# TensorE's order in an expert stage written into the source: whole rounds, additions at two points, alternating accumulator banks, and the group of four experts last

## The chip, the cores and the metric

One core of a Trainium2 chip runs the whole kernel in one launch. The metric is the device time of that core in microseconds (us). Engines are named as the profile names them: PE is TensorE (PEld its weight loads), DVE is VectorE, ACT is ScalarE, POOL is GpSimd, SP is SyncE, which here only issues transfers.

## The reference

One layer of a diffusion backbone works on 256 latent tokens of width 1024: modulation, a combined input projection, a convolution branch, a recurrent branch, a merge, and then a mixture of experts. The change touches the last part alone. A router picks one of four groups for each token and two of the four experts in it, and each of 16 experts is a SwiGLU block (1024 to 512 and back to 1024):

```python
for g in range(N_GROUPS):
    sl = slice(g * EXPERTS_PER_GROUP, (g + 1) * EXPERTS_PER_GROUP)
    hg = jnp.einsum("nd,edf->nef", h, w_gate[sl])
    hu = jnp.einsum("nd,edf->nef", h, w_up[sl])
    act = jax.nn.silu(hg) * hu * combine[:, sl, None]
    out = out + jnp.einsum("nef,efd->nd", act, w_down[sl])
```

`combine` is zero but for a token's two experts. The result is added to the stream, and a final RMSNorm gives the output. Everything is in float32.

## The kernel before

The first 376 us do all that comes ahead of the experts. The expert stage then brings the weights of all 16 experts from HBM once, 16 times 6 MB, and computes with gathered tokens only.

**Groups and parts.** Experts are ranked by their number of tokens, except for experts 8 to 11, which are fixed in the source (`STATIC`) and come first. A group is a set of experts that share one pass: `groups` is the fixed group of four and then what `RANKS` lists by the rank of its first expert. Rank 8 means a group of four experts with 32 token slots each; the others are groups of two. Ranks 0 and 1, the fullest, get 128 slots each and the rest of the pairs 64, so a *part*, one pass over 128 slots, holds 4 x 32 or 2 x 64 slots. The group of ranks 0 and 1 has two parts, which read the same weights; all other groups have one. The order before is: fixed, 0, 8, 6, 2, 4.

**A part.** `up` (line L1228) computes the gate product and then the up product: for each of eight rounds k, the two (four) experts of the group each multiply their 64 (32) slots with a slice of their own weights, side by side in 64 (32) columns of the PE. A *round* is those two or four matmuls; in the trace each is two passes, so a group's gate product is 32 (64) passes. `swiglu` (L1182 to L1184) makes the activation on ACT and DVE, `turned` (L1250) transposes it in four matmuls, ACT copies it to `at` (L1275), and `down` (L1241) multiplies it with the down weights into two banks, one for each half c of the 1024 columns. `to_slots` (L1177) transposes the slot matrix `sg`, and `slot_weights` (L1260) fetches the routing weights. `scatter` makes `yv` (DVE, L1194), `yh` (ACT, L1197) and `yl` (DVE, L1198) for each half, and `add` (L1211, L1212) multiplies them back to the token rows, four matmuls for a half, and adds these to `xt`. The last part has no `yh` and `yl`; its additions are followed by squares for the final norm.

**Gathers.** `slots_of` (DVE, L999) builds the slot matrix, and `gather` fills `hg`, the tokens' columns: two matmuls for the row factors (L1011), 32 for the columns (L1025) through four `misc` banks of which two exist, a multiplication for each bank on DVE (L1029) and two bias additions for each on ACT (L1031). One gather serves ranks 0 and 1, one ranks 2 to 5, one ranks 6 to 11, and one the fixed group.

**Weights.** Each of the 96 halves of an expert matrix is a transfer of 1 MB, here a *chunk*, and goes to one of 18 buffers. The order of the chunks is the order of the groups, within a group gate, up, down, and of each the lower half before the upper. Chunk n waits for the release of the buffer that chunk n - 18 held. `load` is called where the program is done with earlier chunks; SP issues the 24 chunks of the fixed group (L596), POOL the other 72 as indirect transfers (L597), each queue in its order. A chunk of the group with two parts is free only when its second part has read it.

**What sets the order.** The framework's scheduler places the instructions of the expert stage by its own model of time; within an engine the program keeps that place. Only what is passed to `pin` (`tc.keep_in_program_order`) stands in the order of the source, and before this is the router and the fixed group's gather alone. So the scheduler decides where additions of one part fall among the rounds of the next, and where a gather is broken up. Banks: `up` uses `accum(0)` = `acca`, for the second part also `accb`, and `down` always `accb`, two banks each.

The loop at the end of the stage, before:

```python
for p in range(len(groups)):
    if p == 0:
        slots_for(p + 1)
    then = group(p, parts)
    if 0 < p < len(groups) - 1:
        slots_for(p + 1)
    if p + 1 == len(groups):
        gains()
        then()
    else:
        parts = parts_of(p + 1)
        then()
```

`group` runs `up` and `swiglu`, `parts_of` gathers, `then` is the rest of the group (`turned` to `add`); `gains` (L1335) spreads the final norm's factors.

Of the kernel before, what the change touches and what calls it, by code (L numbers as in the profile page):

```python
# [22 lines left out]
CAP = 64  # L23
# [16 lines left out]
RANKS = (0, 8, 6, 2, 4)  # L40
# [5 lines left out]
def hybrid_block(ctx: ExitStack, tc: tile.TileContext, a, out):  # L46
# [959 lines left out]

    def gather(dst, sg, ns, kb, first=False):

        pr = side_bank((128, ns))
        for b in range(2):  # L1010
            ins = T.matmul(pr, r2s[b].to_broadcast([128, 128]), sg[:, b].bitcast(F32), start=(b == 0), stop=(b == 1))  # L1011
            if first:
                pin(ins)
# [6 lines left out]
        for k0 in range(0, 8, kb):  # L1020
            pt = bank("accb", 2, (128, kb, ns)) if first and k0 // kb % 2 else misc((128, kb, ns))
            ks = range(k0, k0 + kb)
            for i, k in [(i, k) for i in range(4) for k in ks] if first else [(i, k) for k in ks for i in range(4)]:
                src, b = terms[i]
                ins = T.matmul(pt[:, k - k0], src[:, b, k, :], sg[:, b], start=(i == 0 and not (first and k > k0)),  # L1025
                               stop=(i == 3 and not (first and k < ks[-1])))
                if first:
                    pin(ins)
# [50 lines left out]
    V.scalar_tensor_tensor(pos, pc[:, 0:2], 1.0, mk16, op0=ALU.add, op1=ALU.mult)  # L1079
    sg0 = slots_of((pos[:, :, STATIC[0]:STATIC[0] + 4], CAP // 2), first=True)  # L1080
# [92 lines left out]
    def to_slots(st, sg):  # L1173

        pst = misc((128, 2, 128))
        for b in range(2):
            T.transpose(pst[:, b, :], sg[:, b].bitcast(F32), ident)  # L1177
# [9 lines left out]
    def scatter(od, st, ws, sums):  # L1187

        yvs = [tmp([128, 512], name="yv") for _ in range(2)] if sums else [None, None]
        for c in range(2):  # L1190
            if not sums:
                yvs[c] = tmp([128, 512], name="yv")
            yv = yvs[c]
            V.scalar_tensor_tensor(yv, od[c], ws, gt2[:, 512 * c:512 * c + 512], op0=ALU.mult, op1=ALU.mult)  # L1194
            if not sums:
# [3 lines left out]
                add(c, [(st, yh), (st, yl)])  # L1199
        if sums:  # L1200
            for c in range(2):
                add(c, [(st.bitcast(F32), yvs[c])])
                for b in range(2):
                    square(b, c)

    def add(c, ops):
        cs = slice(512 * c, 512 * c + 512)
        for b in range(2):
            po = side_bank()
            for i, (s_, y) in enumerate(ops):  # L1210
                T.matmul(po, s_[:, b, :], y, start=(i == 0), stop=(i == len(ops) - 1))  # L1211
            V.tensor_tensor(xt[:, b, cs], xt[:, b, cs], po, op=ALU.add)  # L1212

# [7 lines left out]
    def up(p, ne, key, sls):  # L1221

        o = [accum(j) for j in range(len(sls))]
        n = 128 // ne
        for k in range(8):
            for j, sl in enumerate(sls):
                for i in range(ne):
                    T.matmul(o[j][n * i:n * i + n, :], sl(i, k), wt[p, key, i, k // 4][:, k % 4, :],  # L1228
                             start=(k == 0), stop=(k == 7))
            if k % 4 == 3 and p < 8:  # L1230
                load(ne)
        return o

    def down(p, ne, at, final=True):
# [197 lines left out]
```

## Time and profile before

| what | us |
|---|---|
| median of 3 runs (622.05 to 632.38) | 622.58 |
| the profiled execution, its own time | 620.56 |
| span of the profiled execution, first to last instruction | 618.8 |
| PE busy in that span | 575.0 |
| mean granted PE clock, share of full speed | 0.977 |

The span is what the trace shows, and 1.8 us of the profiled execution's own time lie outside it. Times in the rows below are us from the start of the span. In a row of the timeline the first number is the start, the second the time to the end of the last of its instructions; ends of matmuls are modelled, so the start of the next row says better when one was done. DMA share is the mean busy share of 16 DMA engines.

### The profile page before, as it was taken

The numbers are of one execution on the slowest core, as the hardware profiler recorded it, in microseconds if no ns is written. First come the engines' busy times: TensorE is split into PE (matmuls) and PEld (weight loads), VectorE is DVE, ScalarE is ACT, GpSimd is POOL, SyncE is SP. The second block draws the span as 40 slices with busy tenths as digits, with TensorE's granted clock in tenths as the row PEclk, the third lists the DMA queues.
The fourth block names the chain that finished last, engine by engine and source line by source line (L and its number), as shares of the span: only waits on it lengthen the run. The fifth ranks groups of instructions, "written<-read, shape, count | busy, mean of one in ns | idle before, by whom it ended". The sixth has DMA issues, their size and how long they took to land. (4 is left out here: it accounts for less than half of the span.)

```text
span 618.8 us, 9523 instructions
## 1 busy us (share of the span) xinstructions
PE 575.0 (93%) x3864; PEld 378.5 (61%) x3864; DVE 332.7 (54%) x658; ACT 248.9 (40%) x394; POOL 114.8 (19%) x122
## 2 busy tenths in 40 slices
PE   9989899999999999998999999799899889998980
PEld 8778677767768687798998885523343222533430
DVE  4625884721189978997989657322232431333124
ACT  4316444357946998554856432110030110201112
POOL 0000200010001000224450000433304533333001
PEclk9989899999999999998999999799999999999996
DMA  8983897287562575669867693999996999999801
GB/s 342 421 332 113 299 384 279 82 305 272 184 222 81 205 271 212 253 222 407 332 269 293 261 393 119 423 423 419 420 387 228 428 421 419 421 420 423 365 0 72
DMA packets 31326, 182.86 MB, mean 296 GB/s; under 512 B 3710, under 2 KB 8086, under 8 KB 10796
## 3 DMA queue, kind: packets, MB, share of 16 engines
q1 hardware_dynamic: 18812, 98.21, 41.6%
q0 software_dynamic: 12032, 83.35, 32.8%
q8 instruction: 32, 0.52, 0.3%
q10 hardware_dynamic: 432, 0.62, 0.3%
q14 instruction: 18, 0.15, 0.1%
HBM read 179.53 MB, written 2.64 MB: 294 GB/s over the span
## 5 line engine op out<-in xcount | busy, mean ns | idle before, releaser
L292 DVE TENSOR_TENSOR ws<-raw,ws 128x1024 fp32r<-128x1024 f32 x72 | 92.2, 1302 | 66.1 <-ACT ws L291 66.0
L307 PE MATMUL acca<-hxh,ws 128*128 128x256 f32 (+1 forms) x384 | 106.6, 320 | 2.4 <-ACT hxh L258 2.0
L1228 PE MATMUL acca<-ew,hg 128*32 128x512 f32 (+1 forms) x512 | 107.3, 596 | 0.0
L307 PE MATMUL accb<-hxh,ws 128*128 128x256 f32 (+1 forms) x384 | 99.7, 302 | 0.0
L291 ACT ACTIVATE ws<-raw 128x1024 fp32r<-128x1024 f32 x72 | 74.3, 1053 | 27.5 <-PE accb L307 16.4
L307 PEld LDWEIGHTS acca<-hxh,ws 128*128 128x128 f32 x384 | 68.3, 193 | 17.3 <-issue 10.0
L307 PEld LDWEIGHTS accb<-hxh,ws 128*128 128x128 f32 x384 | 68.2, 193 | 2.9 <-ACT th L388 0.4
L1228 PEld LDWEIGHTS acca<-ew,hg 128*32 128x32 f32 (+1 forms) x512 | 30.8, 123 | 53.8 <-issue 52.2
L1241 PE MATMUL accb<-ew,at 128*64 128x512 f32 (+1 forms) x288 | 52.7, 596 | 3.0 <-ACT at L1275 2.3
L307 PE MATMUL acca<-hxl,ws 128*128 128x256 f32 (+1 forms) x192 | 54.8, 303 | 0.1
L307 PE MATMUL accb<-hxl,ws 128*128 128x256 f32 (+1 forms) x192 | 54.8, 303 | 0.0
L307 PEld LDWEIGHTS acca<-hxl,ws 128*128 128x128 f32 x192 | 36.9, 192 | 4.4 <-issue 2.9
L1212 DVE TENSOR_TENSOR xt<-xt,side 128x512 f32<-128x512 f32 x28 | 18.3, 684 | 38.5 <-PE side L1211 35.5
L1241 PEld LDWEIGHTS accb<-ew,at 128*64 128x64 f32 (+1 forms) x288 | 17.1, 124 | 34.2 <-issue 28.8
L307 PEld LDWEIGHTS accb<-hxl,ws 128*128 128x128 f32 x192 | 37.0, 193 | 1.3
L597 POOL DMA_INDIRECT ew<-in_w_gate_dram,idxd x24 | 22.9, 954 | 70.2 <-PE acca L1228 44.8
L597 POOL DMA_INDIRECT ew<-in_w_down_dram,idxd x24 | 22.5, 936 | 60.6 <-PE acca L1228 23.6
L1197 ACT ACTIVATE yh<-yv 128x512 fp32r<-128x512 f32 x12 | 7.6, 630 | 60.8 <-DVE yv L1194 60.8
L1031 ACT ACTIVATE hg<-hg,sh 128x256 f32<-128x256 f32 (+1 forms) x32 | 13.1, 472 | 46.5 <-DVE hg L1029 46.5
L1194 DVE SCALAR_TENSOR_TENSOR yv<-accb,ws,gt 128x512 f32<-128x512 f32 x14 | 10.5, 748 | 38.2 <-PE accb L1241 38.0
L667 PE MATMUL side<-xc,gw 128*128 128x512 f32 x64 | 30.6, 602 | 0.0
L377 PE MATMUL side<-z,csw 128*32 128x256 f32 x512 | 29.0, 380 | 0.0
(337 smaller groups left out, 981.7 us busy)
## 6 DMA issues: line engine op xcount, KB each, us to landing
raw<-in_w_in_dram SPq DMA_DIRECT2D x24, 1024.0 KB
raw<-in_w_rows_dram SPq DMA_DIRECT2D x16, 1024.0 KB
wsc<-in_w_mod_dram SPq DMA_DIRECT2D x8, 1024.0 KB
ew<-in_w_gate_dram SPq DMA_DIRECT2D x8, 1024.0 KB
ew<-in_w_up_dram SPq DMA_DIRECT2D x8, 1024.0 KB
ew<-in_w_down_dram SPq DMA_DIRECT2D x8, 1024.0 KB
z<-zd POOLq DMA_DIRECT2D x8, 766.0 KB, 9.0
csw<-in_conv_s_dram SPq DMA_DIRECT2D x4, 1024.0 KB
```

The costliest lines, as they stand in the source:

```text
L291: S.activation(w[:, 0], src, AF.Copy)
L292: io(V.tensor_tensor(w[:, 1], src, w[:, 0].bitcast(F32), op=ALU.subtract))
L307: ins = io(T.matmul(o, l[pr[0]], r[pr[1]], start=start and first.get(i) == j and not (paired and i % 2), stop=stop and j >= len(n) - m and ...
L377: T.matmul(o[32 * i:32 * i + 32], csw[t // 2][:, t % 2, i, m], z[:, i, :, 4 * m:4 * m + 64], start=(m == 0), stop=(m == 7))
L597: return P.indirect_dma_start(out=t.rearrange("p k c -> p (k c)"), out_offset=None, in_=wex[key].rearrange("e (r k) c -> (e r) (k c)", k=m ...
L667: T.matmul(o1, gws[g][:, d, m, t], xcs[g][:, t].rearrange("p s n -> p (s n)"), start=True, stop=True)
L1031: S.activation(dst[:, k], dst[:, k], AF.Identity, bias=sh8[:, k:k + 1])
L1194: V.scalar_tensor_tensor(yv, od[c], ws, gt2[:, 512 * c:512 * c + 512], op0=ALU.mult, op1=ALU.mult)
L1197: S.activation(yh, yv, AF.Copy)
L1212: V.tensor_tensor(xt[:, b, cs], xt[:, b, cs], po, op=ALU.add)
L1228: T.matmul(o[j][n * i:n * i + n, :], sl(i, k), wt[p, key, i, k // 4][:, k % 4, :], start=(k == 0), stop=(k == 7))
L1241: T.matmul(od[c][n * i:n * i + n, :], at[:, k, n * i:n * i + n], wt[p, 2, i, h][:, k % 2, 512 * c:512 * c + 512], start=(k == 0), stop=(k ...
```

## The change

`RANKS` becomes 2, 4, 0, 6, 8, so the group with two parts comes fourth instead of second and the group of four last instead of third. From the fixed group's gather on, to the end of the last part, every matmul passes through `fix`, which pins it, so PE runs the stage in the order of the source. That order is new: the two additions of a part (`left`) are taken up at fixed rounds of the next `up`, after rounds 2 and 5 (rounds 1 and 2 where the next group has two parts), or between the quarters of a second part's `down`. `to_slots` and `slot_weights` now come ahead of `turned`. `places_of` alternates the banks: a part's `down` goes to the kind of bank that its `up` did not use (to `misc` ahead of the group with two parts), and the next `up` keeps clear of it. The slot matrix for the next group is built ahead of a group for all groups. Cut to its core:

```diff
-RANKS = (0, 8, 6, 2, 4)
+RANKS = (2, 4, 0, 6, 8)
...
+    fixed = [False]
+
+    def fix(ins):
+
+        return pin(ins) if fixed[0] else ins
...
     def scatter(od, st, ws, sums):
...
+        steps = []
         for c in range(2):
+            yv = tmp([128, 512], name="yv")
             V.scalar_tensor_tensor(yv, od[c], ws, gt2[:, 512 * c:512 * c + 512], op0=ALU.mult, op1=ALU.mult)
-            if not sums:
+            if sums:
+                ops = [(st.bitcast(F32), yv)]
+            else:
                 yh, yl = (tmp([128, 512], F32R, name=n) for n in ("yh", "yl"))
                 S.activation(yh, yv, AF.Copy)
                 V.tensor_tensor(yl, yv, yh.bitcast(F32), op=ALU.subtract)
-                add(c, [(st, yh), (st, yl)])
...
+                ops = [(st, yh), (st, yl)]
+            steps.append((c, ops, sums))
+        return steps
...
+    left = []
+
+    def add_left(n):
+
+        for _ in range(min(n, len(left))):
+            add(*left.pop(0))
...
-    def up(p, ne, key, sls):
+    def up(p, ne, key, sls, o, at=()):
...
             if k % 4 == 3 and p < 8:
                 load(ne)
+            if k in at:
+                add_left(1)
+
+    def down(p, ne, at, od, final=True):
...
+                if 2 * h + c > 0:
+                    add_left(1)
             if final and p < 8:
                 load(ne)
...
+    def finish(p, ne, ac, sg, w, place, final=True, sums=False):
+        st = half([128, 2, 128], F32R, name="st")
+        to_slots(st, sg)
+        ws = slot_weights(sg, w)
         at = tmp([128, 4, 128], name="at")
         S.activation(at, turned(ac, 128), AF.Copy)
-        st = half([128, 2, 128], F32R, name="st")
-        to_slots(st, sg)
-        scatter(down(p, ne, at, final), st, ws, sums)
+        od = [bank(place, 2) for _ in range(2)]
+        down(p, ne, at, od, final)
+        left.extend(scatter(od, st, ws, sums))
...
+        if two:
+            places_of.append((["acca", "accb"], ["accb", "acca"]))
+            free = ["accb", "acca"]
+        else:
+            places_of.append((free[0:1], ["misc" if next_two else free[1]]))
...
     for p in range(len(groups)):
-        if p == 0:
+        if p + 1 < len(groups):
             slots_for(p + 1)
         then = group(p, parts)
-        if 0 < p < len(groups) - 1:
-            slots_for(p + 1)
         if p + 1 == len(groups):
             gains()
-            then()
         else:
             parts = parts_of(p + 1)
-            then()
+        then()
+    add_left(2)
+    fixed[0] = False
```

Three places show what moves. In these rows a name is the tile written, then the tiles read; `ew` are expert weights, `hg` gathered tokens, `side`, `misc`, `acca` and `accb` PSUM banks, and 64x512 or 32x512 tells a group of two from one of four. The order counts matmuls, the trace their passes. The first place is PE where one pair's `down` ends and the next pair's `up` begins, before:

```order
L1241 MATMUL accb<-ew,at 64x512 x16
L1228 MATMUL acca<-ew,hg 64x512 x8
L1211 MATMUL side<-yh,st 128x512 x2
L1211 MATMUL side<-yl,st 128x512 x2
L1228 MATMUL acca<-ew,hg 64x512
L1211 MATMUL side<-yh,st 128x512
L1211 MATMUL side<-yl,st 128x512
L1228 MATMUL acca<-ew,hg 64x512 x7
L1211 MATMUL side<-yh,st 128x512
L1211 MATMUL side<-yl,st 128x512
L1260 MATMUL side<-wd_3828,sg 128x2 x2
L1228 MATMUL acca<-ew,hg 64x512 x16
```

The same place on PE now, in the new line numbers (L1250 is `down`, L1237 is `up`):

```order
L1250 MATMUL accb<-ew,at 64x512 x16
L1237 MATMUL acca<-ew,hg 64x512 x6
L1211 MATMUL side<-yh,st 128x512
L1211 MATMUL side<-yl,st 128x512
L1211 MATMUL side<-yh,st 128x512
L1211 MATMUL side<-yl,st 128x512
L1237 MATMUL acca<-ew,hg 64x512 x6
```

Before, an odd matmul and then seven stand between additions, so two rounds of two are cut in half; now three whole rounds stand ahead of each addition. The second place is PE between the two `down` products of the group with two parts, before:

```order
L1241 MATMUL accb<-ew,at 64x512 x16
L1250 MATMUL misc<-ident,ac 128x128 x4
L1177 MATMUL misc<-ident,sg 128x128 x2
L1228 MATMUL acca<-ew,hg 32x512 x9
L1211 MATMUL side<-yh,st 128x512 x2
L1228 MATMUL acca<-ew,hg 32x512 x4
L1211 MATMUL side<-yl,st 128x512 x2
L1228 MATMUL acca<-ew,hg 32x512 x3
L1241 MATMUL accb<-ew,at 64x512 x11
```

The same place now (L1180 is `to_slots`, L1270 `slot_weights`, L1260 `turned`):

```order
L1250 MATMUL accb<-ew,at 64x512 x16
L1180 MATMUL misc<-ident,sg 128x128 x2
L1270 MATMUL side<-wd_3828,sg 128x2 x2
L1260 MATMUL misc<-ident,ac 128x128 x4
L1250 MATMUL acca<-ew,at 64x512 x8
L1211 MATMUL side<-yh,st 128x512
L1211 MATMUL side<-yl,st 128x512
```

Sixteen matmuls of the next group's gate product stood between the two; none do now, and the first part's additions stand inside the second `down`. The third place is POOL's queue of chunks, before, at the group of four behind the group with two parts:

```order
L597 DMA ew<-in_w_down_dram,idxd 128x2048 x4
L597 DMA ew<-in_w_gate_dram,idxd 128x2048 x8
L597 DMA ew<-in_w_up_dram,idxd 128x2048 x6
L597 DMA ew<-in_w_down_dram,idxd 128x2048 x4
L597 DMA ew<-in_w_up_dram,idxd 128x2048 x2
```

POOL's queue now, from the group with two parts to the end:

```order
L597 DMA ew<-in_w_gate_dram,idxd 128x2048 x4
L597 DMA ew<-in_w_up_dram,idxd 128x2048 x4
L597 DMA ew<-in_w_down_dram,idxd 128x2048 x4
L597 DMA ew<-in_w_gate_dram,idxd 128x2048 x8
L597 DMA ew<-in_w_up_dram,idxd 128x2048 x8
L597 DMA ew<-in_w_down_dram,idxd 128x2048 x8
```

The 24 chunks of the group of four stand last, and no up chunk stands behind a down chunk of its group.

## Rows read from the trace of the kernel before

**Rows 1.** The page, its first line.
```profile
span 618.8 us, 9523 instructions
```

**Rows 2.** Busy time by windows: window and its length, engines, PEclk, DMA share, GB/s.
```profile
476.00:586.00 110.00, 101.31 (x523) 40.25 (x524) 34.88 (x63) 13.60 (x25) 37.72 (x40) 1.00 1.01 420
462.00:476.00 14.00, 14.00 (x74) 4.58 (x70) 3.95 (x8) 1.75 (x3) 5.61 (x6) 1.00 0.48 173
462.00:464.00 2.00, 2.00 (x16) 0.91 (x16) 1.30 (x3) 0.63 (x1) 0.00 (x0) 1.00 0.43 176
470.00:472.00 2.00, 2.00 (x12) 0.65 (x10) 0.00 (x0) 0.00 (x0) 1.52 (x2) 1.00 0.94 250
586.00:588.00 2.00, 2.00 (x12) 0.64 (x10) 0.00 (x0) 0.00 (x0) 0.00 (x0) 1.00 0.14 57
```

**Rows 3.** Timeline of PE at the end: start, us, engine, line, operation, idle before.
```profile
577.50 2.05 PE L1335 MATMUL side<-gf,ident 8*128 8x128 f32 x16
...
600.32 3.89 PE L1211 MATMUL side<-yv,st 128*128 128x512 f32 x8
```

**Rows 4.** Waits of PE from 412 to 601 us: total, times, longest.
```profile
PE side L1011 <- DVE sg L999: 3.9, 2, 2.4
PE misc L1250 <- DVE ac L1184: 3.5, 3, 1.2
PE side L1211 <- DVE xt L1212: 2.1, 2, 1.5
```

**Rows 5.** Timeline of POOL around the gap in its chunks.
```profile
445.54 0.94 POOL L597 DMA_INDIRECT ew<-in_w_up_dram,idxd  x1 [0.75 <-DMA ew<-in_w_gate_dram,idxd]
468.40 0.94 POOL L597 DMA_INDIRECT ew<-in_w_down_dram,idxd  x1 [21.93 <-PE acca L1228]
```

**Rows 6.** Timeline of PE in a group of two experts with one part.
```profile
540.02 3.65 PE L1228 MATMUL acca<-ew,hg 128*64 128x512 f32 x16
543.60 0.73 PE L1211 MATMUL side<-yh,st 128*128 128x512 f32 x2
...
544.73 1.07 PE L1228 MATMUL acca<-ew,hg 128*64 128x512 f32 x2
...
546.40 3.65 PE L1228 MATMUL acca<-ew,hg 128*64 128x512 f32 x14
...
550.97 7.09 PE L1228 MATMUL acca<-ew,hg 128*64 128x512 f32 x32
...
560.53 7.14 PE L1241 MATMUL accb<-ew,at 128*64 128x512 f32 x32 [0.47 <-ACT at L1275]
```

**Rows 7.** Timeline of PE in the group with two parts.
```profile
412.11 1.07 PE L1228 MATMUL acca<-ew,hg 128*64 128x512 f32 x2
...
446.85 0.70 PE L1011 MATMUL side<-sg,r2rsy 128*128 128x256 f32 x2 [2.45 <-DVE sg L999]
...
455.91 7.09 PE L1241 MATMUL accb<-ew,at 128*64 128x512 f32 x32 [0.53 <-ACT at L1275]
...
463.73 2.76 PE L1228 MATMUL acca<-ew,hg 128*32 128x512 f32 x18
...
469.73 5.37 PE L1241 MATMUL accb<-ew,at 128*64 128x512 f32 x22
```

**Rows 8.** Timeline of PE, an unbroken gather and the `down` behind it.
```profile
526.27 0.70 PE L1011 MATMUL side<-sg,r2rsy 128*128 128x256 f32 x2 [1.41 <-DVE sg L999]
...
533.10 7.14 PE L1241 MATMUL accb<-ew,at 128*64 128x512 f32 x32
```

**Rows 9.** Timeline of DVE after the first `down` of the group with two parts.
```profile
461.33 0.75 DVE L1194 SCALAR_TENSOR_TENSOR yv<-accb,ws,gt 128x512 f32<-128x512 f32 x1 [5.49 <-PE accb L1241]
...
464.89 0.69 DVE L1198 TENSOR_TENSOR yl<-yv,yh 128x512 fp32r<-128x512 f32 x1 [0.43 <-ACT yh L1197]
```

**Rows 10.** Busy time by windows in the fixed group's gather, columns as in rows 2.
```profile
393.00:397.00 4.00, 0.10 (x1) 0.01 (x1) 1.93 (x3) 0.00 (x0) 1.50 (x2) 0.77 1.01 420
397.00:400.00 3.00, 2.73 (x13) 2.73 (x14) 1.96 (x7) 1.71 (x4) 0.94 (x1) 0.50 1.02 426
```

More of the change, by code (lines that the diff above doesn't have):

```diff
@@ L1010, in gather @@
         for b in range(2):
-            ins = T.matmul(pr, r2s[b].to_broadcast([128, 128]), sg[:, b].bitcast(F32), start=(b == 0), stop=(b == 1))
-            if first:
-                pin(ins)
+            fix(T.matmul(pr, r2s[b].to_broadcast([128, 128]), sg[:, b].bitcast(F32), start=(b == 0), stop=(b == 1)))
         rb = half([128, ns], name="rb")
@@ L1024, in gather @@
                 src, b = terms[i]
[L1025 to L1028, printed above, removed]
+                fix(T.matmul(pt[:, k - k0], src[:, b, k, :], sg[:, b], start=(i == 0 and not (first and k > k0)),
+                             stop=(i == 3 and not (first and k < ks[-1]))))
             gathered_at[0] = V.tensor_tensor(dst[:, k0:k0 + kb], pt, rb[:, None].to_broadcast([128, kb, ns]), op=ALU.mult)
@@ L1198, in scatter, with add @@
                 V.tensor_tensor(yl, yv, yh.bitcast(F32), op=ALU.subtract)
-                add(c, [(st, yh), (st, yl)])
[L1200 to L1206, printed above, removed]
+                ops = [(st, yh), (st, yl)]
+            steps.append((c, ops, sums))
+        return steps
+    def add(c, ops, sums):
         cs = slice(512 * c, 512 * c + 512)
@@ L1259, in slot_weights @@
         for b in range(2):
-            T.matmul(pw, sg[:, b].bitcast(F32), w[:, b], start=(b == 0), stop=(b == 1))
+            fix(T.matmul(pw, sg[:, b].bitcast(F32), w[:, b], start=(b == 0), stop=(b == 1)))
         for i in range(ne):
@@ L1293, in extra_pair @@
             load_chunk(8, *c[1:], idx=idx)
-        finish(8, 2, run(8, 2, [columns(hg, 0, C2, CAP)])[0], s2, ws, sums=True)
+        finish(8, 2, run(8, 2, [columns(hg, 0, C2, CAP)], ["acca"])[0], s2, wd, "accb", sums=True)
+        add_left(2)
+    free, places_of = ["acca", "accb"], []
+    for p, (kind, r, _) in enumerate(groups):
+        two = (kind, r) == ("d", 0)
+        next_two = p + 1 < len(groups) and groups[p + 1][0:2] == ("d", 0)
+        if two:
[3 more added lines that the diff above has]
+            places_of.append((free[0:1], ["misc" if next_two else free[1]]))
     def group(p, parts):
@@ L1299, in group @@
         w = (wst if kind == "s" else wd12)[:, :, r:r + ne]
-        acs = run(p, ne, [columns(hg, c, 128 // ne, 128 // ne) for _, hg, c in parts])
+        first, later = places_of[p]
+        acs = run(p, ne, [columns(hg, c, 128 // ne, 128 // ne) for _, hg, c in parts], first,
+                  (1, 2) if len(parts) > 1 else (2, 5))
         def rest():
             for j, (sg, _, c) in enumerate(parts):
-                sl = sg[:, :, c:c + 128]
-                finish(p, ne, acs[j], sl, slot_weights(sl, w), j == len(parts) - 1,
+                finish(p, ne, acs[j], sg[:, :, c:c + 128], w, later[j], j == len(parts) - 1,
                        p + 1 == len(groups) and j == len(parts) - 1)
```

42 lines of the change are left out of this document (19 added, 23 removed).

## The prediction

> **What bounds the kernel now.** I read the page's first line, then the windows of the expert stage, then who waits for whom there. Only this stage changes; it runs from 376 us to the end of the span of 618.8 us [rows 1].
>
> Two streams run side by side in it. The first is the transfers: from 476 to 586 us their share is 1.01 at 420 GB/s [rows 2], so a chunk (1024 KB) takes 1.049 MB / 420 GB/s = 2.50 us, and nothing can make that stream shorter but fewer gaps. There is one gap: in the 14 us from 462 to 476 the rate is 173 GB/s [rows 2], which loses 14 x (1 - 173/420) = 8.2 us. Its cause is in POOL's timeline: behind the chunk issued at 445.54 the next is issued at 468.40, 21.93 us later, released by a PE matmul [rows 5]. All 18 buffers were full and PE had not read the next one. The stream ends in the window 586 to 588, where the share is 0.14 [rows 2]; I count 588.0 as its end.
>
> The second stream is PE. Its last additions start at 600.32 [rows 3], so it runs about 12.3 us behind the last chunk. The waits of PE in 412 to 601 us are short: 3.9 us for slot matrices, 3.5 for the activation, 2.1 for an addition's bank [rows 4]. So at the end PE is the bound, by its work and its order, and the transfers are done 12 us earlier; from 462 to 470 us PE holds up the transfers too. From 600.3 to 618.8 the additions, the branch, the norm and the output take 18.5 us; the change leaves those as they are.
>
> **The change part by part.** First the prices, all at the full clock (1.00, 2.4 GHz, in all windows of rows 2).
>
> *Whole rounds.* Fourteen passes, seven matmuls, take 3.65 us, as do sixteen [rows 6]: half a round of two costs a whole one, 0.44 us. Two such halves in this group vanish. A part's `up` becomes two products of 7.09 us and two additions. One addition's four matmuls take 544.73 - 543.60 = 1.13 us, switches between the widths included [rows 6]. That is 14.2 + 2.3 = 16.4 us.
>
> *From `up` to `down`.* 550.97 + 7.09 = 558.06, and `down` starts at 560.53 [rows 6]: 2.5 us. The slot transposes and weights, which now stand ahead of `turned`, fit in the wait for the activation. With a gather between them it is 533.10 - 526.27 = 6.8 us [rows 8]; the wait of 1.41 us ahead of it (2.45 in rows 7) goes, since the slot matrix is built a group earlier on a DVE that idles. `down` is 7.1 us [rows 6]. A group of four costs the same per part: its rounds have four matmuls of half the width.
>
> *The walk.* Up to 412.1 us, where the fixed group's `down` ends [rows 7], I see no difference. Then:
> - ranks 2 and 3: 16.4 + 2.5 + 7.1 = 26.0, to 438.1;
> - ranks 4 and 5, with a gather: 16.4 + 6.8 + 7.1 = 30.3, to 468.4;
> - ranks 0 and 1, two parts: `up` 28.4 + 2.3 = 30.7; gather 6.8, and 0.8 because a second activation stands ahead of it on DVE; `down` 7.1; then 2.4 us to the second `down` (ACT's copy now stands behind both `yh`: the second `yl` starts at 464.89, 1.9 us after the first `down` ends at 455.91 + 7.09 [rows 7, 9], and the copy takes about half a us); the second `down` with two additions 7.1 + 2.3 = 9.4. Together 57.2, to 525.6, and the second `down` starts at 516.2;
> - ranks 6 and 7: 26.0, to 551.6;
> - the group of four: `up` 16.4, to 568.0; the gains 2.05 [rows 3], to 570.1, which hide the activation; 2.5 to `down`, at 572.5; its lower half 3.6, to 576.1.
>
> *The transfers.* The gap is a matter of the two-part group, whose chunks come free only in its second `down`. That group starts 24 chunks later in the stream, so the buffers run dry 24 x 2.50 = 59.9 us later: the share of 0.43 in 462 to 464 puts the dry point at 462.9 [rows 2], now 522.8. The first chunks come free 3.3 us into the second `down`, at 519.5. Issue to first data took from 468.40 [rows 5] to 470.1 (a share of 0.94 in 470 to 472 [rows 2]), 1.7 us; so data flow at 521.5, before the dry point. The next pair comes free at 525.4, data at 527.4, needed at 522.8 + 5.0 = 527.8. Both margins are about a us, so I take 1.0 us of gap in place of 8.2 (bounds below). POOL's order, with no up chunk behind a down chunk, costs nothing, as its issues are paced by the stream. The last chunk lands at 588.0 - 8.2 + 1.0 = 580.8.
>
> *The sum.* PE stands ready at 576.1 and the last chunk comes at 580.8, so the transfers decide: 580.8 + 3.6 (upper half of `down`) + 18.5 = 602.9 us of span, against 618.8. With 1.8 us outside the span, 604.7 against the profiled execution's 620.56: 15.9 us less. The median of the runs shown, 622.58, is 2.0 above that execution, and I forecast on its scale: 606.7.
>
> *What I cost at nothing, and bounds.* The additions are now fixed in PE's queue, with all later rounds behind them. The first `yv` starts at 461.33; the second `yl` ends at 465.58, 2.6 us after that `down` [rows 7, 9]. They are wanted three rounds (2.7 us) after `down` for the first half, whose `yl` is ready at about 0.5, and 6.4 us after for the second. Without this cover each would cost up to 2.1 us, one link of `yv`, `yh`, `yl`. Nothing is gained here below zero. The alternating banks remove a wait for `yv` that these rows do not show; I give them nothing, with 0 to 2 us of gain, which would fall in PE's 4.7 us of slack. A gather inside PE's fixed order costs at least the 6.8 us of rows 8, which I take, being unbroken like the new one, and at most the 455.91 - 446.85 = 9.1 us of rows 7, which had foreign rounds in it; two lie ahead of the gap, so up to 4.6 us more. Low end: no gap, and the 0.28 us of work in 586 to 588 [rows 2] done by 586.3, leaves PE as the bound: 576.1 + 3.6 + 18.5 + 1.8 + 2.0 = 602.0. SP's read of the spill count moves behind the last two fixed chunks; nothing waits for it before the final branch.
>
> **The rivals.**
>
> *The gap moves with the group.* For it: that group starts with the same lead, the stream some four chunks ahead of it, as before. If its second `down` begins as late in it as before, 469.73 - 412.11 = 57.6 us instead of 47.8 [rows 7], buffers come free at 529.3 and data flow at 531.3: a gap of 8.5 us, 9.5 with the restart. That is 615.2; half of the delay gives some 610.5 to 611. Against it: six us of that stretch are another group's rounds (463.73 to 469.73 [rows 7]) and 2.45 a wait, and neither is in the new order.
>
> *The clock falls in the last group.* In the new order PE is ahead of the transfers at the end and each round needs all four experts' chunks. In the fixed group's gather PE was busy 0.10 of 4 us, the granted clock fell to 0.77 for that window and to 0.50, the 1.2 GHz level, for the next 3 us [rows 10]. If that happens in the 4.7 us before 580.8, the last half `down` costs 3.6 us more and the additions, 3.9 us now [rows 3], about one: 611.3. Against it: chunks arrive singly, so PE has a matmul every 2.5 us. The Trainium skill ("TensorE: Matmul & The Clock Gate", section "HAM oscillation — how this bites in real kernels") says that where a burst of matmuls is over before its next transfer lands, the clock falls in the wait and the next burst starts slow. By that rule the time would be this rival's 611.3 and not 606.7; rows 10 agree with it for a wait for DVE, and no row shows one of single matmuls.
>
> *The fixed additions stall PE: slower than before.* In the old order rounds could fill in; now everything stands behind an addition that is not ready. There are 12 points (six parts, two each). From 1.3 us a point the gain of 15.9 is gone; at the full 2.1 us of a link each, 25 us less the 4.7 of slack, the time is 627. For it: one addition waited 1.5 us for its bank before [rows 4]. Against it: the margins above, 2.2 and 3.8 us.
>
> **How the numbers follow.** The forecast's case, 602 to 610, gets 0.62; the gap that moves, 610 to 615, 0.20; the clock, 611, 0.12; stalled additions, about 627 and up to 640, 0.06. Two per cent of 622.58, about what a measurement of this kernel can tell from no change, is 12.5, so faster means below 610.1: that is the forecast's case, 0.62. The two middle rivals and half of the last are within 2%: 0.34; slower keeps 0.04. The range runs from 601.5 to 615.5; it takes in both middle rivals and leaves out the last.
>
> **What would show it.** Right: a share near 1.01 from 410 to about 580 us with no window of 2 us under a half; POOL without a wait of over 10 us behind the group with two parts; that group some 57 us long and single pairs 26; PE waiting for chunks in the last `down`; the last additions at 584 to 585 us. Wrong: a gap near 523 us (first rival), 0.50 granted behind 576 us (second), PE waits for `yh` or `yl` in sum over 5 us (third), or PE still ten us behind the last chunk, which would mean that the walk leaves out work of PE.

## The result, and the profile after

The changed kernel took 604.73 us (median of 4 runs, 603.39 to 607.34) beside 622.32 for the kernel before on the same chip: a ratio of 0.9726, 95% interval 0.9684 to 0.9768. That is faster. The ratio comes from the single runs, without one slow run of before (632.38 us), and so is not quite the quotient of the two medians. On two more chips it took 603.98 beside 619.11 and 603.90 beside 619.23 (0.9745 and 0.9752). The profiled execution took 605.15 us. The page, against [rows 1]:

```profile
span 603.3 us, 9530 instructions
...
PE 562.9 (93%) x3864; PEld 371.7 (62%) x3864; DVE 332.1 (55%) x658; ACT 249.1 (41%) x394; POOL 115.5 (19%) x122
```

The span is 15.5 us shorter, PE's work 12.1. The windows of the expert stage, against [rows 2] (span of time, its length, busy time of PE, PEld, DVE, ACT and POOL, granted clock, DMA share, GB/s):

```profile
376.00:410.00 34.00, 29.08 (x231) 12.06 (x234) 13.41 (x56) 6.77 (x19) 11.40 (x12) 0.92 0.87 354
405.00:411.00 6.00, 4.17 (x20) 0.99 (x24) 0.51 (x1) 0.00 (x0) 1.88 (x2) 0.50 1.02 425
410.00:516.00 106.00, 101.93 (x502) 42.50 (x494) 35.14 (x64) 16.46 (x32) 36.45 (x39) 0.99 1.01 421
518.00:540.00 22.00, 22.00 (x98) 8.07 (x96) 8.54 (x13) 1.86 (x3) 8.44 (x9) 1.00 0.95 357
...
572.00:574.00 2.00, 2.00 (x12) 0.57 (x16) 0.00 (x0) 0.00 (x0) 0.00 (x0) 0.50 0.98 401
...
578.00:580.00 2.00, 1.19 (x4) 0.14 (x2) 0.00 (x0) 0.00 (x0) 0.00 (x0) 1.00 0.66 274
580.00:582.00 2.00, 0.77 (x8) 0.29 (x12) 0.00 (x0) 0.00 (x0) 0.00 (x0) 1.00 0.02 8
```

The hole of 173 GB/s is gone. What is left of it lies between 518 and 540 us: 22 x (1 - 357/421) = 3.3 us, where the forecast was 1.0. The last chunk is in just behind 580 us (a share of 0.02 in 580 to 582; the DMA view has its last bytes at 580.4, and at 587.9 before), forecast 580.8. The clock fell twice, in the fixed group's `down` (0.50 at 405 to 411) and behind the gains (0.50 at 572 to 574).

PE's timeline, against [rows 3, 6 and 7]: the end of the fixed group, the starts of `down` and of the next `up`, and the last group.

```profile
406.83 5.95 PE L1250 MATMUL accb<-ew,at 128*32 128x512 f32 x26 [3.92 <-DMA ew<-in_w_down_dram]
412.72 2.79 PE L1237 MATMUL acca<-ew,hg 128*64 128x512 f32 x12
...
431.72 7.09 PE L1250 MATMUL accb<-ew,at 128*64 128x512 f32 x32 [0.69 <-ACT at L1291]
...
469.15 1.03 PE L1237 MATMUL acca<-ew,hg 128*64 128x512 f32 x4
...
506.73 7.09 PE L1250 MATMUL accb<-ew,at 128*64 128x512 f32 x32 [0.76 <-ACT at L1291]
...
516.22 3.65 PE L1250 MATMUL acca<-ew,at 128*64 128x512 f32 x16 [1.19 <-ACT at L1291]
...
525.68 2.75 PE L1237 MATMUL accb<-ew,hg 128*64 128x512 f32 x12
...
544.63 7.09 PE L1250 MATMUL acca<-ew,at 128*64 128x512 f32 x32 [0.69 <-ACT at L1291]
...
568.04 2.05 PE L1363 MATMUL side<-gf,ident 8*128 8x128 f32 x16
...
571.98 6.17 PE L1250 MATMUL acca<-ew,at 128*32 128x512 f32 x36 [0.69 <-ACT at L1291]
578.78 1.04 PE L1250 MATMUL acca<-ew,at 128*32 128x512 f32 x2 [0.63 <-DMA ew<-in_w_down_dram,idxd]
581.23 3.62 PE L1250 MATMUL acca<-ew,at 128*32 128x512 f32 x26 [1.41 <-DMA ew<-in_w_down_dram,idxd]
584.78 3.89 PE L1211 MATMUL side<-yv,st 128*128 128x512 f32 x8
```

This is the walk of the prediction, step by step: the two-part group starts at 469.15 (forecast 468.4), its second `down` at 516.22 (516.2), ranks 6 and 7 at 525.68 (525.6), the gains at 568.04 (568.0), the last `down` at 571.98 (572.5), the last additions at 584.78 (584.4). One step differs: the lower half of the last `down` was to be done at 576.1, but at the fallen clock 36 passes took 6.17 us, to 578.1. PE now waits for the last two chunks (578.78 and 581.23), and its last additions start 4.4 us behind the last bytes instead of 12.4. POOL's timeline, against [rows 5]:

```profile
503.64 0.94 POOL L597 DMA_INDIRECT ew<-in_w_gate_dram,idxd  x1 [1.53 <-PE misc L1029]
520.14 0.94 POOL L597 DMA_INDIRECT ew<-in_w_gate_dram,idxd  x1 [15.55 <-PE acca L1250]
...
526.12 0.94 POOL L597 DMA_INDIRECT ew<-in_w_gate_dram,idxd  x1 [3.80 <-PE acca L1250]
...
530.82 0.94 POOL L597 DMA_INDIRECT ew<-in_w_gate_dram,idxd  x1 [2.53 <-PE accb L1237]
```

The wait is still there, 15.55 us in place of 21.93, but the stream lives on its lead through nearly all of it. PE's waits from 412 to 601 us, against [rows 4]:

```profile
PE acca L1250 <- ACT at L1291: 2.6, 3, 1.2
PE acca L1250 <- DMA ew<-in_w_down_dram,idxd: 2.0, 2, 1.4
```

No wait for a slot matrix, and none for `yv`, `yh`, `yl` or `xt`.

### The profile page after: what moved, and what is told of

It reads as the page before. It is cut to its first block, busy times and chain, and to the rows that moved or that the text cites. A ratio compares the mean times of both kernels' runs of the same rounds, so it can differ in the third digit from the quotient of the medians.

```text
span 603.3 us, 9530 instructions
## 1 busy us (share of the span) xinstructions
PE 562.9 (93%) x3864; PEld 371.7 (62%) x3864; DVE 332.1 (55%) x658; ACT 249.1 (41%) x394; POOL 115.5 (19%) x122
## 5 line engine op out<-in xcount | busy, mean ns | idle before, releaser
L1237 PE MATMUL acca<-ew,hg 128*64 128x512 f32 (+1 forms) x320 | 59.2, 595 | 0.0
L1237 PE MATMUL accb<-ew,hg 128*64 128x512 f32 (+1 forms) x256 | 45.1, 594 | 0.0
L1237 PEld LDWEIGHTS acca<-ew,hg 128*64 128x64 f32 (+1 forms) x320 | 17.2, 126 | 35.5 <-issue 34.5
L1250 PE MATMUL accb<-ew,at 128*32 128x512 f32 (+1 forms) x128 | 25.7, 675 | 6.2 <-DMA ew<-in_w_down_dram 3.9
L597 POOL DMA_INDIRECT ew<-in_w_down_dram,idxd x24 | 22.8, 951 | 36.3 <-issue 12.4
L1250 PE MATMUL acca<-ew,at 128*64 128x512 f32 (+1 forms) x128 | 25.4, 654 | 4.6 <-ACT at L1291 2.6
L1237 PEld LDWEIGHTS accb<-ew,hg 128*64 128x64 f32 (+1 forms) x256 | 12.8, 123 | 27.2 <-issue 27.2
```

The costliest lines, as they stand in the source:

```text
L597: return P.indirect_dma_start(out=t.rearrange("p k c -> p (k c)"), out_offset=None, in_=wex[key].rearrange("e (r k) c -> (e r) (k c)", k=m ...
L1237: fix(T.matmul(o[j][n * i:n * i + n, :], sl(i, k), wt[p, key, i, k // 4][:, k % 4, :], start=(k == 0), stop=(k == 7)))
L1250: fix(T.matmul(od[c][n * i:n * i + n, :], at[:, k, n * i:n * i + n], wt[p, 2, i, h][:, k % 2, 512 * c:512 * c + 512], start=(k == 0), stop ...
```

## The experiments

The theory: the gain is the shorter way to the two-part group's second `down` (less gap) and PE's catching up with the stream at the end. The rivals: the order of the groups alone brings it; the fixed order alone (here: all of the change but `RANKS`); the banks; and whether PE or the stream now sets the end. "After" below means its runs on the chip named with it. Runs 1 to 4 were on a chip on which after had not run, so against them its times come from other chips.

**1. The order of groups alone.**

```diff
 # kernel before
-RANKS = (0, 8, 6, 2, 4)
+RANKS = (2, 4, 0, 6, 8)
```

> The kernel before with RANKS = (2, 4, 0, 6, 8) alone: the same order of groups as after, but TensorE's instructions placed by the scheduler. My theory: the gain comes from the time between the start of the two-part group and its second `down`, and an order of ranks cannot shorten that. In the scheduler's order of this kernel a gather and most of the next pair's `up` rounds stand between the two-part group's first `up` and its second `down`, so I expect that `down` some 62 to 64 us into the group (57.6 before, 47.1 after). Its first chunks then come free about 11 us behind the point at which the 18 buffers run dry, the stream has a gap of 13 to 14 us, and the last chunk lands near 592 us; with 3.6 for the upper half of the last `down`, 18.5 to the end and 1.8 outside the span that is 616 us (612 to 620). Rival, the new order of groups brings the gain and the fixed order within them little: 609 us or less, with a gap under 5 us.

Measured 622.77 us (10 runs) beside 618.74: a ratio of 1.0065 (1.0041 to 1.0090), so 4 us slower than before and some 19 slower than after. PE's timeline from the group's start, then POOL's:

```profile
475.95 3.65 PE L1228 MATMUL acca<-ew,hg 128*64 128x512 f32 x16
...
526.76 7.40 PE L1241 MATMUL accb<-ew,at 128*64 128x512 f32 x31
...
543.44 4.45 PE L1241 MATMUL accb<-ew,at 128*64 128x512 f32 x18
...
595.09 7.11 PE L1241 MATMUL accb<-ew,at 128*32 128x512 f32 x64 [0.53 <-ACT at L1275]
```

```profile
537.97 0.94 POOL L597 DMA_INDIRECT ew<-in_w_up_dram,idxd  x1 [8.22 <-PE acca L1228]
...
564.80 0.94 POOL L597 DMA_INDIRECT ew<-in_w_down_dram,idxd  x1 [10.58 <-PE acca L1228]
```

The scheduler put the second `down` 543.44 - 475.95 = 67.5 us into the group, not 62 to 64. The windows show 326 GB/s at 520 to 530, 229 at 530 to 540, 390 at 540 to 560 and 291 at 560 to 580 us: 2.3 + 4.6 + 1.5 + 6.2 = 14.6 us lost. The sum is near the theory's 13 to 14, but it is not the theory's one gap: 6.9 to 8.4 us of it lie around the second `down` and 6.2 behind it, where POOL waited 10.58 us for rounds of the next group. The rest of the miss (622.77 is 2.8 us above the range) is at the end: the last `down` starts at 595.09, just behind the last bytes (594.8), and runs whole, 7.1 us, so PE too was late. The rival falls.

**2. The fixed order alone.**

```diff
 # kernel after
-RANKS = (2, 4, 0, 6, 8)
+RANKS = (0, 8, 6, 2, 4)
```

> The kernel after with RANKS = (0, 8, 6, 2, 4): the old order of groups, TensorE's order fixed in the source as after. My theory: the group with two parts is as short as after wherever it stands, and the gap depends on the stream's lead at that place. Its second `down` starts 47 us behind the end of the fixed group's `down`, at about 460; its first chunks come free at 463.7 where the buffers run dry at 461.5, so the gap is about 5 us in place of about 3. PE has the same work in all and is not the bound. The last chunk lands near 582.8 us and the time is 606.5 us (605 to 608). Rival, the place of the two-part group and of the group of four is what brings the most of the gain of 17 us: 612 us or more, with a gap of 8 us as before.

608.15 us beside 618.74 (0.9823, 0.9781 to 0.9866): most of the gain, 10.6 of some 15. Rates and PE's end:

```profile
458.00:480.00 22.00, 22.00 (x145) 7.29 (x140) 8.55 (x13) 1.86 (x3) 10.24 (x11) 1.00 0.89 332
```

```profile
572.59 3.65 PE L1237 MATMUL accb<-ew,hg 128*64 128x512 f32 x14 [0.72 <-DMA ew<-in_w_up_dram,idxd]
...
580.10 7.09 PE L1250 MATMUL acca<-ew,at 128*64 128x512 f32 x32 [0.69 <-ACT at L1291]
587.12 3.89 PE L1211 MATMUL side<-yv,st 128*128 128x512 f32 x8
```

The gap is 22 x (1 - 332/421) = 4.7 us, as the theory said. But it missed the end: with a pair last, PE waits for an *up* chunk and then for nothing; the whole `down` lies behind 580.10 and the additions at 587.12, 0.7 us later than the theory's 582.8 + 3.6. Against after (604 to 604.7, on other chips) that is 3.4 to 4.1 us, where 1.8 was expected; the sign and the order were right, the time stands 0.15 us outside the range.

**3. The two-part group second, the group of four last.** `RANKS = (0, 2, 4, 6, 8)` in the kernel after.

> The kernel after with RANKS = (0, 2, 4, 6, 8): the group of four stays last, the group with two parts comes second as before. It tells the place of the two-part group (against after) from the place of the group of four (against the run with the old order of groups). My theory: as with the old order of groups, a gap of about 5 us near 462 us and 606.5 us (605 to 608); the place of the group of four is worth nothing, within 1 us, because its part costs PE the same. Rival, the group of four at the end costs PE time (its rounds want four experts' chunks): this run is 2 us or more slower than the run with the old order of groups.

607.37 us (0.9797, 0.9758 to 0.9835): as expected, and not slower than run 2. The rate at 458 to 480 us was 331 GB/s, a gap of 4.7 us as in run 2. So it is most likely the place of the two-part group, with less lead early in the stream, that is worth some 3 us (after on other chips), and the group of four costs nothing at the end. Its profile shows the clock's price:

```profile
583.30 5.09 PE L1250 MATMUL acca<-ew,at 128*32 128x512 f32 x26 [1.41 <-DMA ew<-in_w_down_dram,idxd]
```

```profile
584.00:586.00 2.00, 2.00 (x16) 0.54 (x12) 0.00 (x0) 0.00 (x0) 0.00 (x0) 0.50 0.00 0
```

Twenty-six passes took 5.09 us at 0.50, which took 3.62 at full clock after.

**4. The next gather behind the second `down`.**

```diff
+        late = len(parts) > 1
...
-        else:
+        elif not late:
             parts = parts_of(p + 1)
         then()
+        if late:
+            parts = parts_of(p + 1)
```

> The kernel after, but the gather for ranks 6 and 7 moved from between the two-part group's `up` and first `down` to behind its second `down`. My theory: the second `down` starts 7 us earlier (509 in place of 516.2 us), so its first chunks come free 7 us earlier and the small loss of transfer after 520 us (324 GB/s from 520 to 530 us after, which loses about 2.3 us) shrinks; but the gather now stands ahead of the next group's rounds, whose first chunks come free later, near 532 us, so that part of the loss comes back there. I expect the last chunk 0 to 2 us earlier and 604 us (602.5 to 605.5). Rival, the loss after 520 us is not a matter of buffers that come free late but of the issue on POOL: the same loss at 520 to 530 us, and a time equal to after within 0.5 us.

602.51 us beside 618.74 (0.9732, 0.9692 to 0.9771). The second `down` and the rate:

```profile
508.33 3.65 PE L1250 MATMUL acca<-ew,at 128*64 128x512 f32 x16 [1.19 <-ACT at L1291]
```

```profile
518.00:540.00 22.00, 22.00 (x114) 10.85 (x114) 8.30 (x13) 4.79 (x10) 6.85 (x8) 1.00 1.01 416
```

The loss there is 22 x (1 - 416/421) = 0.3 us. The rival asked for the same loss at 520 to 530 us; at 518 to 530 us the rate is 420 GB/s, against 340 in the first profile of after. The issue on POOL is thus not its cause; buffers that come free late are. Both kernels then ran on another chip, together with runs 8 and 9:

> The kernel after, unchanged, beside the next three on the same chip. Both theories expect a ratio to before of 0.974 (0.970 to 0.978) and some 602 to 605 us.

> The kernel with the late gather once more, now with after beside it on the same chip. In its first profile the last chunk landed at 577.4 us, against 580.7 and 579.3 in two profiles of after, and the group's second `down` came 7 us earlier. My theory: what after still loses between 519 and 540 us is a matter of buffers that come free late, and that loss is 1.7 to 3.8 us; with it gone the kernel is 1 to 3 us faster than after. Rival, an end fixed by a straggling part of the last chunk and by the clock in the last `down`, which differ from run to run, hides it: within 0.7 us of after.

After took 603.90 us (0.9752, 0.9719 to 0.9785), this one 602.78 (0.9719, 0.9685 to 0.9753). It has the lower median, by 1.1 us, at the theory's edge; the intervals overlap, so that it beats after is likely and not shown. Its profile this time lost more (374 GB/s at 518 to 540 us, 2.5 us), nearly all of it behind the second `down`, at the first rounds of the next group, where the theory of run 4 said that loss could come back:

```profile
530.00:540.00 10.00, 10.00 (x48) 3.51 (x46) 1.97 (x3) 0.60 (x1) 4.97 (x6) 1.00 0.89 321
```

```profile
530.34 0.94 POOL L597 DMA_INDIRECT ew<-in_w_gate_dram,idxd  x1 [8.93 <-PE accb L1237]
```

In the first profile POOL waited as long there (8.94 us), but 2.2 us earlier, because the fixed group's `down` had ended at 410.33 and not at 412.55.

**5 to 7. Cut rounds, banks, and the place of the additions**, each alone, beside after on one chip.

> The kernel after, unchanged, beside the next three on the same chip, so that effects of 1 to 5 us can be read against it. Two chips so far gave the kernel before at 622 and 619 us. Both theories expect a ratio to before of 0.973 (0.969 to 0.977), and the same trace as after within 1 us: second `down` of the two-part group 47 us behind that group's start, a loss of transfer of some 3 to 4 us between 519 and 540 us.

```diff
 # run 5, in up
+                    if k - 1 in at and i == 0 and j == 0:
+                        add_left(1)
...
-            if k in at:
-                add_left(1)
 # run 6, places_of
-            places_of.append((["acca", "accb"], ["accb", "acca"]))
-            free = ["accb", "acca"]
+            places_of.append((["acca", "accb"], ["accb", "accb"]))
...
-            places_of.append((free[0:1], ["misc" if next_two else free[1]]))
+            places_of.append((free[0:1], free[1:2]))
 # run 7, in run
+        add_left(2)
-        up(p, ne, 0, sls, og, at)
+        up(p, ne, 0, sls, og)
```

> The kernel after, but each addition ahead of the two-part group's second `down` and later is taken up behind the first matmul of a round in place of a round's end, so that round is cut in two. The work is the same. My theory: a cut round costs a whole round more, 0.44 us; six addition points lie ahead of the group's second `down`, so that `down` starts 2.6 us later, its chunks come free 2.6 us later and the last chunk lands 2.6 us later: 2 to 3 us more than the unchanged kernel beside it. The points behind that are covered by the wait for chunks and cost nothing. Rival, a cut round costs nothing, since TensorE's next matmul is queued anyway: within 0.7 us of the unchanged kernel.

> The kernel after without the alternating banks: `up` always in acca (and accb for the second part), `down` always in accb, as before the change. The order of TensorE's instructions stays. My theory: the banks of a part's `down` are read by DVE within 2.6 us of its end and the next use of that kind is a whole `up` later, so single pairs lose nothing; in the two-part group `up` writes accb three rounds in, near the time at which the `down` ahead of it is read, and the second `down` wants accb while the first one's is read, which can cost up to 2 us there. I expect 0 to 2 us more than the unchanged kernel, 1 us as the likeliest. Rival, the alternation carries the change: 4 us or more, with waits of TensorE for `yv` in each group.

> The kernel after, but both additions of a part stand at the very start of the next `up`, with no round ahead of them. The work is the same. My theory: TensorE then waits for the chain `yv`, `yh`, `yl`, about 0.5 us for the first half and 1 us for the second; three groups lie ahead of the two-part group's second `down`, so it starts about 4.5 us later (3 to 5), and the last chunk lands as much later: 3 to 5 us more than the unchanged kernel, with waits of TensorE for `yh` or `yl` of 1 to 2 us for each group in the trace. Rival, where the additions stand is without weight because the whole chain is done by the end of `down`: within 0.7 us of the unchanged kernel and no such waits.

After 603.98 us (0.9745, 0.9711 to 0.9779); cut rounds 604.58 (0.9752, 0.9724 to 0.9781); same banks 603.66 (0.9729, 0.9698 to 0.9759); additions at once 609.06 (0.9815, 0.9786 to 0.9844). The start of the second `down` in the four, in this order:

```profile
513.57 3.65 PE L1250 MATMUL acca<-ew,at 128*64 128x512 f32 x16 [1.19 <-ACT at L1291]
```

```profile
410.02 3.65 PE L1237 MATMUL acca<-ew,hg 128*64 128x512 f32 x14
...
515.99 3.65 PE L1250 MATMUL acca<-ew,at 128*64 128x512 f32 x16 [1.19 <-ACT at L1291]
```

```profile
513.52 3.65 PE L1250 MATMUL accb<-ew,at 128*64 128x512 f32 x16 [1.19 <-ACT at L1291]
...
579.10 4.98 PE L1250 MATMUL accb<-ew,at 128*32 128x512 f32 x26 [1.41 <-DMA ew<-in_w_down_dram,idxd]
```

```profile
519.37 3.65 PE L1250 MATMUL acca<-ew,at 128*64 128x512 f32 x16 [1.19 <-ACT at L1292]
```

```profile
PE side L1211 <- DVE yl L1201: 3.7, 8, 0.6
...
PE side L1211 <- ACT yh L1200: 2.1, 5, 0.4
```

Cutting costs PE what the theory said: fourteen passes take 3.65 us again (410.02), the second `down` comes 2.4 us later (theory 2.6), and the loss at 518 to 540 us grows from 0.9 to 2.9 us (403 and 365 GB/s). Yet the time grows by 0.6 us only, less than the 2 to 3 expected and within the rival's 0.7, and the intervals overlap: PE's work shows the cost, the time does not. The last additions too come 0.6 us later (583.97 against 583.36): the bulk of the last chunk comes 1.8 us later, but its tail is shorter in this profile, as the DMA view in the last section shows. But PE, at 0.50 from 573 to 579 us, runs through that `down` in 10.41 us without a wait for a chunk, so which of the two set the end there is not shown, and one profile does not explain the medians: why run 5 costs so little stays open. The banks are worth nothing that shows, the low end of the theory; no wait for `yv` came up. The additions' place is worth 5.1 us, at the upper end of what was expected (3 to 5); the second `down` comes 5.8 us later, and the waits for `yl` and `yh` are back, 5.8 us in sum. Here the rival falls: the chain is not done when `down` ends.

**8 and 9. More TensorE work, and a pair at the end.**

```diff
 # run 8, in the loop
         if p + 1 == len(groups):
             gains()
+            idle = side_bank()
+            for _ in range(16):
+                fix(T.matmul(idle, ...
 # run 9
-RANKS = (2, 4, 0, 6, 8)
+RANKS = (2, 4, 0, 8, 6)
```

> The kernel after with 16 more matmuls behind the gains in the last group, into a bank that nobody reads: some 3.5 us more of TensorE work directly ahead of the last `down`. My theory: the last chunk sets the end, and TensorE waits for chunks in the last `down` (1.4 to 2 us in sum in the profiles, and some 1.2 to 2.5 us more of it went by at the half clock), so the additional work falls into the wait: 0 to 1 us more than after; and since TensorE does not idle there its clock should fall less often. Rival, TensorE still sets the end, as it did before the change: 3 us or more.

> The kernel after with RANKS = (2, 4, 0, 8, 6): the group of four and the last pair change places, nothing else. Behind a pair's last `up` chunk only four chunks follow (10 us of stream), behind that of the group of four eight (20 us). My theory: with a pair at the end TensorE has to do half of the up product, gains, transposes and half of `down` (about 3.6 + 2.0 + 1.9 + 3.6 = 11 us) in the 10 us between the last `up` chunk and the last chunk, so it stands 0.5 to 2 us behind the last chunk: 0 to 2 us slower than after, with a wait of TensorE for an up chunk in the last group and none for a down chunk. Rival, the group of four at the end costs time since each of its rounds wants four chunks: 1 us or more faster than after.

After 603.90 us; run 8 603.07 (0.9734, 0.9698 to 0.9769); run 9 606.48 (0.9788, 0.9752 to 0.9824).

```profile
574.00 4.49 PE L1250 MATMUL acca<-ew,at 128*32 128x512 f32 x38 [0.69 <-ACT at L1291]
579.32 3.62 PE L1250 MATMUL acca<-ew,at 128*32 128x512 f32 x26 [0.83 <-DMA ew<-in_w_down_dram,idxd]
```

```profile
569.45 3.65 PE L1237 MATMUL accb<-ew,hg 128*64 128x512 f32 x14 [0.21 <-DMA ew<-in_w_up_dram,idxd]
...
576.97 8.78 PE L1250 MATMUL acca<-ew,at 128*64 128x512 f32 x32 [0.69 <-ACT at L1291]
585.68 3.89 PE L1211 MATMUL side<-yv,st 128*128 128x512 f32 x8
```

The additional work moves the last `down` to 574.00 and costs nothing: PE no longer sets the end. The granted clock was 1.00 throughout 566 to 588 us in this one profile. With a pair last the wait is for an up chunk and none for a down chunk, as the theory said; 2.6 us slower than after, just over its 2, with intervals that overlap a little; in the profile the clock fell in `down` (0.51 at 577 to 580 us), which took 8.78 us in place of 7.09 and can be 1.7 us of it. So the group of four most likely belongs at the end, where eight chunks follow the last `up` chunk and PE has time to stand ready; between runs 2 and 3, which also differ in the group that comes last, the difference was 0.8 us.

## Why the prediction was right, and where it was off

**The sum** held: 602.9 us of span forecast, 603.3 measured; 604.7 for the profiled execution, 605.15 measured. The term that did not is the 2.0 us added for the median's scale: after's median lies 0.4 us below its profiled execution, so 606.7 was 2.0 too high. That the rest fits to 0.4 us is partly luck, as the next paragraphs show.

**The walk** held within 0.8 us at every step up to the last `down`, and so did the durations under it. The durations are the sound part: from the two-part group's start to its second `down` all three profiles of after have 47.1 us (47.8 forecast). That the times fit too is partly luck: in two other executions of after the fixed group's `down`, from which the walk starts, ended 2.6 and 4.4 us earlier. Runs 5 and 7 show two of the prices by their opposite: a cut round costs PE 0.40 us (2.4 / 6; 0.44 forecast), and the three rounds ahead of an addition cover the chain that would otherwise stall PE. The banks at nothing were right (run 6).

**The gap** was mis-sized: 3.3 us in this execution, where 1.0 was forecast with both margins "about a us" (the forecast's own figures give 1.3 and 0.4). The stream began earlier (354 GB/s at 376 to 410 us, 335 before: 34 x 19 / 421 = 1.5 us), so the dry point came at about 521.3, not 522.8. The forecast put that at nothing, but it goes with the fixed order: its 12 profiles have 351 to 381 GB/s in that window, the two in the scheduler's order (before and run 1) 335 and 332; why was not looked into. The first chunks came free 3.9 us into the second `down`, in all three profiles of after, and not 3.3, a figure that no row showed. The first pair was issued at 520.14, data 1.7 us later at 521.8; the second at 526.12, data at 527.8 where 526.8 was needed. That explains 0.5 + 1.0 = 1.5 us. For the other 1.8 the cause stays open: the third pair, issued at 530.82, was in time, and from 530 to 540 us the rate was still 378 GB/s. In two other executions of after the group began 2.6 and 4.4 us earlier and the same window ran at 403 GB/s, a loss of 0.9 us. Run 4 shows that an earlier second `down` closes the gap at 518 to 530 us (420 and 418 GB/s in its two profiles; 340, 404 and 399 in those of after), but not what follows at 530 to 540 us. In the profiles of after and of runs 4, 5, 6 and 8, which keep the order of groups, the loss at 518 to 540 us goes with the time at which the next group's rounds begin: 0.3 to 1.4 us where that was before 523.2 us, 2.5 to 3.3 where it was after 525.1. So the first release alone does not set the gap; the pairs behind it, freed by the next group's rounds, count as well.

Three misses nearly cancel, and by luck: the early start of the stream (-1.5), the larger gap (+2.3) and the shorter tail of the last chunk (-1.2: the rate runs down for 1.5 us, for 2.7 in the profile of before; see the last section). They leave 580.8 - 0.4 = 580.4, where the last bytes landed. The ledger of the 15.5 us: 1.5 at the start of the stream, 8.3 - 3.3 = 5.0 in the gap (262 GB/s at 458 to 480 us before), 1.2 in the tail, 12.4 - 4.4 = 8.0 in PE's distance behind the last bytes; the sum, 15.7, is 0.2 too much.

**The rivals.** The gap did not move with the group: 47.1 us to the second `down`, against 57.6. In the scheduler's order it did, and grew (run 1), so that rival named the right danger. Stalled additions did not come, but run 7 gives their price when they do: 5.1 us, and 5.8 us of waits in sum, where the forecast allowed up to 25 us (12 points of 2.1). The falling clock did come, in 10 of the 12 profiles of kernels with the fixed order, between 569 and 586 us. Its price was mis-sized: where it met the last half of `down`, in three of them, that half took 5.0 to 5.2 us for 3.6, some 1.5 us and not the 4.6 of the forecast; where it met the lower half, the wait for chunks hid it in after, but in runs 5, 7 and 9 PE had no wait for chunks left in `down` to hide it. It can be seen at the wait of 3.92 us in the fixed group's `down` too: the clock fell to 0.50 within that wait (405 to 411 us), and the second part took 5.95 us for 3.6. There the trace agrees with the Trainium skill ("TensorE: Matmul & The Clock Gate", section "HAM oscillation — how this bites in real kernels"), by which a burst that runs out of data meets a fallen clock when the data come. The fall at 572 us followed the gains and transposes, not a wait for data, as in seven of the ten profiles; in the three in which it met the last half it came after waits of 1.3 to 1.5 us for single chunks, which is the rival's case.

**What I said would show it** held but for two signs. The share fell to 0.95 at 518 to 540 us, 0.81 in the worst window of 2 us (520 to 522): the first rival's gap at its place, though small. And POOL waited: "none over 10 us" was a bad sign to pick. From the last issue ahead of a wait the stream lived 462.9 - 445.54 = 17.4 us, so a wait of 15.55 and an issue cost next to nothing while 21.93 cost 8.2.

**What the parts are worth** (chips with before near 619 us): order of groups alone +4.0, fixed order alone -10.6, both -15.1 to -15.3. They are not additive: a late two-part group helps only if its second `down` comes early in it. What the fixed order's share is made of is shown in part only: run 7 prices the place of the additions, run 5 whole rounds, run 6 the banks. The slot matrix built a group earlier (3.9 us of waits for it before [rows 4]), the slot transposes ahead of `turned` and the unbroken gathers were not tried alone.

## What to carry to other kernels

Where a stream of weights runs through a ring of buffers, find the group that holds its buffers longest and count the time from its start to its first release; the order of the groups moves the gap, the order of instructions within that group shortens it. Count the releases behind the first too: where they come late, the loss comes back there. When two streams run side by side, price what each would take alone behind the last transfer: once PE had caught up, more PE work (some 4 us) cost nothing, and a last group with few chunks behind its `up` cost 0.8 to 2.6 us. Give additions that hang on a chain over other engines a few rounds of cover, and check by which wait the end is set before counting a gain of any other.

## What was not expected of the hardware

The last chunk has a tail. The DMA view from 570 to 582 us, in slices of 0.3 us, of after beside run 5 and then of run 5 itself:

```profile
GB/s 355 410 410 382 382 382 437 437 437 437 410 410 437 437 410 437 437 410 410 410 382 219 137 82 55 55 55 27 27 27 0 0 0 0 0 0 0 0 0 0
```

```profile
GB/s 437 437 437 437 382 437 437 437 410 437 382 410 410 410 437 410 464 410 410 437 355 410 410 410 437 410 410 273 246 137 82 55 0 0 0 0 0 0 0 0
```

In after the full rate ends at 576.3 us; then it falls in steps, at the end to a sixteenth (27 of 437 GB/s), which I read as one of the 16 engines, until 579.0, and PE goes on at 579.80. In run 5 the full rate ends 1.8 us later, at 578.1, but the last bytes land at 579.6: tails of 2.7 and 1.5 us. The tail was 1.5, 2.7 and 1.8 us in the three profiles of after, so a short one is not an effect of run 5's delay. The Trainium skill ("DMA: Bandwidth & Descriptors", section "Why a DMA increments its semaphore by 16 and not by 1") says that the engines of one transfer finish independently and that it counts as landed when all have; the trace agrees, as PE goes on only behind the last bytes. Why the tail is longer in one run than in another was not tried. In the first profile of after the rate also dipped at 533.5 to 535 us (191 to 328 GB/s), with the third pair issued in time; whether that is the same thing is not shown.

The stage's start differs between executions of one kernel: the fixed group's `down` ended at 412.72, 410.07 and 408.28 us in three profiles of after. In the first the half clock met the wait in that `down` and its second part, in the second the gather, in the third the gather and the first part of `down`. The third also began its transfers earlier (421 GB/s at 380 to 385 us, 285 and 316 in the others). The gap was 3.3, 0.9 and 0.9 us.
